# One-hot and gate rows of the expert layers in float16 pairs, built on VectorE alone

## The chip, the cores and the metric

The kernel runs on one NeuronCore of a Trainium2 chip. The metric is device time in microseconds, the median of the runs. TensorE (PE in the profile) multiplies matrices into PSUM; VectorE (DVE), ScalarE (ACT) and GpSimd (POOL) work on SBUF tiles of 128 partitions, the first two on PSUM too; SyncE (SP) issues the loads of the weights. Each engine takes its instructions in one fixed order and waits at semaphores for the others.

## The reference, cut to what matters

The program is a stack of a dozen phases over 256 tokens of width 1024: feed-forward layers, four kinds of attention and state-space mixers, and, twice, a layer of 16384 experts. The change lies in the two expert layers alone:

```python
def peer_ffn(x, norm_g, q_w, sub_keys, u, v):
    ...
    h = rmsnorm(x, norm_g).reshape(T, D)
    q = (h @ q_w).reshape(T, PEER_HEADS, 2, PEER_HALF)
    s = jnp.einsum('thcd,ckd->thck', q, sub_keys).astype(jnp.float32)
    s1, i1 = lax.top_k(s[:, :, 0], PEER_TOPK)
    s2, i2 = lax.top_k(s[:, :, 1], PEER_TOPK)
    cand_s = (s1[..., :, None] + s2[..., None, :]).reshape(T, PEER_HEADS, PEER_TOPK * PEER_TOPK)
    cand_i = (i1[..., :, None] * N_KEYS + i2[..., None, :]).reshape(T, PEER_HEADS, PEER_TOPK * PEER_TOPK)
    best_s, best_pos = lax.top_k(cand_s, PEER_TOPK)
    idx = jnp.take_along_axis(cand_i, best_pos, axis=-1)
    gate = jax.nn.softmax(best_s, axis=-1).astype(x.dtype)
    ...
        a = jnp.einsum('nd,nhkd->nhk', hb, u[ib])
        w = gb * jax.nn.gelu(a, approximate=False)
        return jnp.einsum('nhk,nhkd->nd', w, v[ib])
```

For each token, 8 heads choose 16 experts each out of 128 x 128, and the gated gelu of the token's product with row `u` of an expert weighs row `v` of it.

## The kernel before

The weights stream in once, in units of 128 x 1024 float32. SP loads a unit into a buffer `raw`; ACT rounds it to float32r (`whi`, L189) and DVE takes the remainder (`wlo`, L190), so that three matmuls give a product of nearly float32 precision. `Stream.conv` does both, and a unit's field `eng` can put the remainder on another engine: in each expert layer `peer_units` sets it to GpSimd for 24 units (`us[LO0:LO1:LOS]`, every second one of units 24 to 71).

The experts are not gathered. The layer computes gelu(h . u) for all 16384 experts, multiplies by a dense gate (zero for an expert that was not chosen), and multiplies by all of v. `W[i1, i2, token]`, with i1 on the partitions, holds the gated values; it lies in three tiles, `Wa` (i2 0 to 63), `Wc` (64 to 79) and `Wb` (80 to 127), with the 256 tokens innermost. What happens in a layer, in the order of the code:

- 16 units of the query weights are multiplied (`chunk_t`), and x scaled by the norm's factor is transposed for the expert products (`scaled`, the tile `hn`).
- `u_pair(i)` takes two units, 24 matmuls of 256 columns for each (L1672 to L1674), then a gelu on ACT. 58 such pairs run with background work beside them, four more after it, ahead of and among the products with v. If some tokens' gates are there already, the gelu goes to a tile `ga` and `flush` (L1661) multiplies it into `W`; for the other tokens it is written to `W`.
- Beside these products runs the generator `search()`, the background work. `half_scores` finds the 16 best keys per half and head (MAX8, FIND_INDEX8 and MATCH_REPLACE8 on DVE); `choose` forms the candidates, finds the 16 best and softmaxes them, and turns the chosen i1, i2 and the gates so that (head, rank) lies on the partitions and tokens along the free axis (`key2`, `gate2`); `gates` builds the dense gates. For a pair of tokens it compares a row 0 to 127 with both keys (`eq`, L1588: 512 float16 values in a partition: key half, token, place) and multiplies the one-hot row of i1 by both parts of the gate (`A`, split into a float16 and the remainder). Of the four pairs in eight tokens, `HOT = "gaga"` gives the first and third product `A` to GpSimd (one instruction, L1600), the second and fourth to ACT (four instructions, L1597). Two matmuls a token, `A` times the one-hot row of i2 (L1607), give the token's 128 x 128 gates in PSUM. For eight tokens at a time `meet` multiplies those into the gelu values that are in `W` (DVE, L1575), or writes them where no gelu is yet (ACT, L1578).

What stands around what is set by credits. Each unit of `u_pair` calls `tick(UTICK)`, which runs the generator until its yielded weights have used up the credit. DVE keeps the order of the code up to the end of `choose` (a region of manual schedule); after that, and on the other engines throughout, a scheduler places instructions by its own estimates within the limits of the data and of buffers (four `eq`, four `A`, four `raw`). After the 58 pairs `drain_bg` runs what is left of the generator.

Of the kernel before, what the change touches and what calls it, by code (L numbers as in the profile page):

```python
# [33 lines left out]
# columns of the per-partition parameter tile  # L34
# [11 lines left out]
# rows of the parameters that are spread over the partitions  # L46
# [29 lines left out]
HOT = "gaga"  # L76
# the gates are split into float16 parts at this scale
# [33 lines left out]
class Stream:  # L111
    """the weights in the order of their use: loaded ahead, then split into float32r parts ahead.
    A phase that has room lends a pool for more parts; its last units always lie there, so that the
    first ones of the next phase can be split before the last ones of this are used up"""
# [38 lines left out]
    def place(self, u):  # L153
        """the pool for the parts of u, or None when there is no room yet"""
# [42 lines left out]
    def take(self, n=1, conv=True):  # L197
        """the next n units, held until the next call"""
# [15 lines left out]
class HTs:  # L214
    """blocks of eight in several tiles"""
# [8 lines left out]
class Next:  # L224
    """the transposed normed x for a phase, in hi and lo parts, without the tokens' factors r"""
# [15 lines left out]
    def trans(self, t):  # L241
        """pairs of blocks alternate between two banks, which the splits take in turns"""
# [27 lines left out]
class Kern:  # L270
# [34 lines left out]
    def tri(self, pool, name, dtype, n, keep, other, base, step, mult):  # L305
        """value keep where mult*partition + step*free + base >= 0, else other"""
# [25 lines left out]
    def split(self, src, shape, tag, pool, bufs=1):  # L332
        """hi and lo parts of src, each exact in float32r"""
# [16 lines left out]
    def rstd(self, out, ss, n, eps, mul=1.0, ms=None):  # L350
        """mul * (ss / n + eps) ** -0.5; ms is for what is raised to the power"""
# [16 lines left out]
    def begin(self, pool):  # L368
        """the transposed normed x of this phase; its first token tile is prepared by now"""
# [47 lines left out]
    def second(self, nx, pool):  # L417
        """the second token tile of the norm"""
# [29 lines left out]
    def chunk_n(self, acc, ht, units, kb0, nk, t, cols):  # L448
        """natural orientation: acc[:, t, :cols] gets h[t] @ W"""
# [10 lines left out]
    def nat(self, acc, ht, cols, head=None, mid=None, tick=0):  # L460
        """natural orientation, a chunk of four units with two k-blocks each"""
# [17 lines left out]
    def wide(self, accs, ht, nk, head=None, mid=None, tail=None):  # L479
        """accs[t][:, half, :] gets h[t] @ W for the 1024 columns of W; units hold one k-block"""  # L480
# [32 lines left out]
    def chunk_t(self, acc, ht, nk, kb0, units):  # L513
        """transposed orientation: acc[:, b // 2, (b % 2) * 256 :] = (h @ W_b)^T for four blocks b"""
# [15 lines left out]
    def log_exp_table(self):  # L530
        """the table with both functions, loaded once the last activation noted is issued"""
# [6 lines left out]
    def traced(self):  # L538
        """the instruction traced last"""
# [1446 lines left out]
```

## Time and profile before

| | |
|---|---|
| time, median of 3 runs (lowest, highest) | 3185.92 us (3181.03, 3186.96) |
| span of the profiled execution | 3172.1 us |
| busy: PE, DVE, ACT, POOL | 3031.7, 2231.7, 1724.8, 541.6 us |
| first expert layer: first key search to its last gate | 1270 to 1735 us of the span |
| second expert layer, the same | 2285 to 2746 us |

The profile's span is from the first to the last instruction on the core; the device time has some 14 us more around it. Busy times are unions of records on an engine; a share near 100% in a stretch says that the engine has no gap there. All times in the traces are from the span's start.

### The profile page before, as it was taken

The numbers are of one execution on the slowest core, as the hardware profiler recorded it, in microseconds if no ns is written. First come the engines' busy times: TensorE is split into PE (matmuls) and PEld (weight loads), VectorE is DVE, ScalarE is ACT, GpSimd is POOL, SyncE is SP. The second block draws the span as 40 slices with busy tenths as digits, with TensorE's granted clock in tenths as the row PEclk, the third lists the DMA queues.
The fourth block names the chain that finished last, engine by engine and source line by source line (L and its number), as shares of the span: only waits on it lengthen the run. The fifth ranks groups of instructions, "written<-read, shape, count | busy, mean of one in ns | idle before, by whom it ended". The sixth has DMA issues, their size and how long they took to land. (4 is left out here: it accounts for less than half of the span.)

```text
span 3172.1 us, 48810 instructions
## 1 busy us (share of the span) xinstructions
PE 3031.7 (96%) x18398; PEld 2625.6 (83%) x18398; DVE 2231.7 (70%) x3555; ACT 1724.8 (54%) x2976; POOL 541.6 (17%) x391
## 2 busy tenths in 40 slices
PE   8999999999999999988988999998998898999998
PEld 7888888887888988988988888886898888888886
DVE  5555655547655776999998555567699999855555
ACT  5446545437545656445766444456544676544444
POOL 0000000002000012133665000001123466400000
PEclk9999999999999999999999999999999999999999
DMA  7653555653554544544444666664354444566664
GB/s 228 184 185 110 179 185 186 186 168 107 180 184 140 176 123 133 162 145 149 139 132 134 187 187 187 188 182 150 109 160 146 148 135 133 154 188 189 186 186 149
DMA packets 142221, 513.66 MB, mean 162 GB/s; under 512 B 16672, under 2 KB 17312, under 8 KB 141984
## 3 DMA queue, kind: packets, MB, share of 16 engines
q1 hardware_dynamic: 138816, 504.16, 52.1%
q10 hardware_dynamic: 3168, 6.37, 0.6%
q8 instruction: 144, 2.36, 0.3%
q14 instruction: 93, 0.76, 0.1%
HBM read 509.42 MB, written 1.05 MB: 161 GB/s over the span
## 5 line engine op out<-in xcount | busy, mean ns | idle before, releaser
L190 DVE TENSOR_TENSOR wlo<-raw,whi 128x1024 fp32r<-128x1024 f32 x912 | 1164.8, 1281 | 547.5 <-ACT whi L189 546.1
L189 ACT CAST whi<-raw 128x1024 fp32r<-128x1024 f32 x962 | 1001.9, 1046 | 697.6 <-PE tr L1673 199.7
L1674 PE MATMUL tr<-hs,wlo 128*128 128x256 f32 x1984 | 566.6, 286 | 39.4 <-DVE wlo L190 39.4
L1672 PE MATMUL tr<-hs,whi 128*128 128x256 f32 x1984 | 574.8, 290 | 5.8 <-DVE gate L1554 4.5
L1673 PE MATMUL tr<-hs,whi 128*128 128x256 f32 x1984 | 563.1, 284 | 0.0
L1674 PEld LDWEIGHTS tr<-hs,wlo 128*128 128x128 f32 x1984 | 377.4, 190 | 44.8 <-DVE wlo L190 44.8
L328 PE MATMUL acc<-whi,wh 128*128 128x512 f32 x1024 | 406.0, 396 | 0.0
L330 PE MATMUL acc<-whi,wl 128*128 128x512 f32 x1024 | 405.9, 396 | 0.0
L329 PE MATMUL acc<-wlo,wh 128*128 128x512 f32 x1024 | 405.9, 396 | 0.0
L1672 PEld LDWEIGHTS tr<-hs,whi 128*128 128x128 f32 x1984 | 379.2, 191 | 7.0 <-issue 3.7
L1673 PEld LDWEIGHTS tr<-hs,whi 128*128 128x128 f32 x1984 | 379.3, 191 | 0.1
L328 PE MATMUL acc<-whi,ht 128*128 128x512 f32 (+2 forms) x832 | 330.1, 397 | 3.8 <-ACT ht L258 3.8
L329 PE MATMUL acc<-wlo,ht 128*128 128x512 f32 (+2 forms) x832 | 326.6, 393 | 1.2 <-DVE wlo L190 1.1
L330 PE MATMUL acc<-whi,ht 128*128 128x512 f32 (+2 forms) x832 | 325.8, 392 | 0.0
L1600 POOL TENSOR_TENSOR A<-eq,gate 128x512 f16<-128x512 f16 x128 | 239.8, 1883 | 206.8 <-DVE eq L1588 197.4
L330 PEld LDWEIGHTS acc<-whi,wl 128*128 128x128 f32 x1024 | 192.9, 188 | 47.0
L329 PEld LDWEIGHTS acc<-wlo,wh 128*128 128x128 f32 x1024 | 192.9, 188 | 46.9
L328 PEld LDWEIGHTS acc<-whi,wh 128*128 128x128 f32 x1024 | 192.9, 188 | 46.8
L1588 DVE TENSOR_TENSOR eq<-iof,key 128x512 f16<-128x512 f16 x256 | 204.3, 833 | 20.2 <-PE acc L1607 19.1
L328 PEld LDWEIGHTS acc<-whi,ht 128*128 128x128 f32 x832 | 157.1, 189 | 37.8 <-ACT ht L258 4.6
L1597 ACT ACTIVATE A<-eq,gate 128x128 f16<-128x128 f16 x512 | 163.1, 393 | 46.4 <-DVE eq L1588 46.2
L329 PEld LDWEIGHTS acc<-wlo,ht 128*128 128x128 f32 x832 | 157.1, 189 | 35.9 <-DVE wlo L190 3.2
(430 smaller groups left out, 4955.2 us busy)
## 6 DMA issues: line engine op xcount, KB each, us to landing
raw<-in_peer_u_dram SPq DMA_DIRECT2D x256, 512.0 KB, 3.6
raw<-in_peer_v_dram SPq DMA_DIRECT2D x256, 512.0 KB, 3.6
raw<-in_ffn_in_dram SPq DMA_DIRECT2D x176, 512.0 KB, 3.6
raw<-in_ffn_out_dram SPq DMA_DIRECT2D x88, 512.0 KB, 3.5
raw<-in_ssm_zx_dram SPq DMA_DIRECT2D x48, 512.0 KB, 3.6
raw<-in_peer_q_dram SPq DMA_DIRECT2D x32, 512.0 KB, 3.7
raw<-in_sb_qk_dram SPq DMA_DIRECT2D x16, 512.0 KB, 4.5
raw<-in_ssm_out_dram SPq DMA_DIRECT2D x16, 512.0 KB, 3.6
```

The lines of the kernel that those rows point to most:

```text
L189: nc.scalar.copy(hi[:, : u.n], raw[:, : u.n])
L190: (u.eng or nc.vector).tensor_tensor(lo[:, : u.n], raw[:, : u.n], hi[:, : u.n].bitcast(F32), ALU.subtract)
L328: mm(out, lh, rh, start=start, stop=False, skip_group_check=True)
L329: mm(out, lh, rl, start=False, stop=False, skip_group_check=True)
L330: mm(out, ll, rh, start=False, stop=stop, skip_group_check=True)
L1588: v.tensor_tensor(eq, iof.unsqueeze(1).unsqueeze(1).broadcast_to([P, 2, 2, P]), key2[:, :, n : n + 2].unsqueeze(3).broadcast_to([P, 2, 2, P]),
L1597: nc.scalar.activation(A[:, i, k, :], eq[:, 0, i, :], AF.Copy, scale=gate2[:, k, n + i : n + i + 1])
L1600: (nc.gpsimd if way == "g" else v).tensor_tensor(A, eq[:, 0].unsqueeze(2).broadcast_to([P, 2, 2, P]), gate2[:, :, n : n + 2].rearrange("p ...
L1672: mm(out, u.hi[:, k, :], hs.hi[:, k, :], start=k + b == 0, stop=False, **kw)
L1673: mm(out, u.hi[:, k, :], hs.lo[:, k, :], start=False, stop=False, **kw)
L1674: mm(out, u.lo[:, k, :], hs.hi[:, k, :], start=False, stop=k == KD - 1, **kw)
```

## The change

`key2` and `gate2` become one float16 tile `kg` of four rows (both keys, both parts of the gate). The one-hot tiles get the two tokens of a pair innermost: `[2, 128 places, 2 tokens]`, so the keys and gates are read as runs of two neighbouring float16 values, no longer as one value repeated along the row. All `A` products are on DVE, and so are the remainders of the 24 units, the multiplication in `flush`, and `hn`. The matmuls read `A` and `eq` with a step of two values. `meet` runs with the tokens innermost: `W` is touched in runs of eight float32 values, and PSUM is read with a step of 128 values. The weights that pace the generator are new: `UTICK` 1.3 to 2.0, and other yields throughout.

```diff
-UTICK = 1.3
-MEET = lambda nc: nc.gpsimd
-GW = 2.6
-CW = 1.0
-HOT = "gaga"
+UTICK = 2.0
+GW = 3.9
...
-        for u in us[LO0:LO1:LOS]:
-            u.eng = self.nc.gpsimd
...
-            key2 = p.tile([P, 2, S], F16, name="key2")
-            gate2 = p.tile([P, 2, S], F32, name="gate2")
+            kg = p.tile([P, 4, S], F16, name="kg")
...
-                            yield 0.9
+                            yield 1.65
...
-                            yield CW * 0.9
+                            yield 1.4
...
-                            yield CW * 0.9
+                            yield 2.0
...
-                            yield CW * 0.9
+                            yield 1.0
...
-                    v.tensor_copy(key2[:, :, ts], tr[:, 0:256].rearrange("p (a b) -> p a b", a=2))
-                    gh = tk.tile([P, P], F16, tag="gh", bufs=1, name="gh")
-                    v.tensor_scalar(gh, tr[:, 256:384], GSCALE, None, ALU.mult)
-                    v.tensor_copy(gate2[:, 0, ts], gh)
-                    v.scalar_tensor_tensor(gate2[:, 1, ts], tr[:, 256:384], GSCALE, gh,
+                    v.tensor_copy(kg[:, 0:2, ts], tr[:, 0:256].rearrange("p (a b) -> p a b", a=2))
+                    v.tensor_scalar(kg[:, 2, ts], tr[:, 256:384], GSCALE, None, ALU.mult)
+                    v.scalar_tensor_tensor(kg[:, 3, ts], tr[:, 256:384], GSCALE, kg[:, 2, ts],
...
-                iof = hot.tile([P, P], F16, name="iof")
+                iof = hot.tile([P, P, 2], F16, name="iof")
...
-                    gv = gp.rearrange("p h (n i) -> p (h n) i", i=P)
+                    gv = gp.rearrange("p h (n i) -> p i (h n)", i=P)
...
-                            w = W(b0, m)[:, :, ns].rearrange("p i n -> p n i")
-                            v.scalar_tensor_tensor(w, gv[:, :, b0:m], 1 / GSCALE, w, ALU.mult,
+                            w = W(b0, m)[:, :, ns]
+                            v.scalar_tensor_tensor(w, gv[:, b0:m, :], 1 / GSCALE, w, ALU.mult,
                                                    ALU.mult)
...
-                        eq = hot.tile([P, 2, 2, P], F16, tag="eq", bufs=NB, name="eq")
+                        eq = hot.tile([P, 2, P, 2], F16, tag="eq", bufs=NB, name="eq")
                         v.tensor_tensor(
-                            eq, iof.unsqueeze(1).unsqueeze(1).broadcast_to([P, 2, 2, P]),
-                            key2[:, :, n : n + 2].unsqueeze(3).broadcast_to([P, 2, 2, P]),
+                            eq, iof.unsqueeze(1).broadcast_to([P, 2, P, 2]),
+                            kg[:, 0:2, n : n + 2].unsqueeze(2).broadcast_to([P, 2, P, 2]),
                             ALU.is_equal)
-                        A = hot.tile([P, 2, 2, P], F16, tag="A", bufs=NA, name="A")
...
-                                    nc.scalar.activation(A[:, i, k, :], eq[:, 0, i, :], AF.Copy,
-                                                         scale=gate2[:, k, n + i : n + i + 1])
...
-                            (nc.gpsimd if way == "g" else v).tensor_tensor(
-                                A, eq[:, 0].unsqueeze(2).broadcast_to([P, 2, 2, P]),
...
+                        A = hot.tile([P, 2, P, 2], F16, tag="A", bufs=NA, name="A")
+                        v.tensor_tensor(
+                            A, eq[:, 0].unsqueeze(1).broadcast_to([P, 2, P, 2]),
+                            kg[:, 2:4, n : n + 2].unsqueeze(2).broadcast_to([P, 2, P, 2]),
+                            ALU.mult)
...
-                                mm(o, A[:, i, k, :], eq[:, 1, i, :], start=k == 0, stop=k == 1,
+                                mm(o, A[:, k, :, i], eq[:, 1, :, i], start=k == 0, stop=k == 1,
...
-                nc.gpsimd.tensor_scalar(hs.src[t], self.x[:, t, :], ht.r[:, t : t + 1], None,
+                v.tensor_scalar(hs.src[t], self.x[:, t, :], ht.r[:, t : t + 1], None,
...
-                    MEET(nc).tensor_tensor(w, ga, w, ALU.mult)
+                    v.tensor_tensor(w, ga, w, ALU.mult)
```

The order that the built programs have shows the move at three places. On DVE, in `choose`, for one head of the second token tile before (wlo is a unit's remainder, eq<-pf,io the comparison that looks up the chosen ranks; `eq<-iof` further down is the one-hot row):

```order
L190 TENSOR_TENSOR wlo<-raw,whi 128x1024
L1509 MAX best<-cs 128x8
L1510 MAX_INDEX pu<-best,cs 128x8
L1511 MATCH_REPLACE c_13279<-best,cs 128x50
L1512 MAX best<-c_13279 128x8
L1513 MAX_INDEX pu<-best,c_13279 128x8
L1514 CAST pf<-pu 128x16
L1517 TENSOR_TENSOR eq<-pf,io 128x800
L1520 TENSOR_TENSOR eq<-eq,ci 128x800
L1525 TENSOR_REDUCE idx<-eq 128x16
L190 TENSOR_TENSOR wlo<-raw,whi 128x1024
```

and after:

```order
L182 TENSOR_TENSOR wlo<-raw,whi 128x1024
L1515 TENSOR_REDUCE idx<-eq 128x16
L182 TENSOR_TENSOR wlo<-raw,whi 128x1024
L1499 MAX best<-cs 128x8
L1577 TENSOR_TENSOR eq<-iof,kg 128x512
L1500 MAX_INDEX pu<-best,cs 128x8
L1501 MATCH_REPLACE c_13811<-best,cs 128x50
L1582 TENSOR_TENSOR A<-eq,kg 128x512
L1502 MAX best<-c_13811 128x8
L1503 MAX_INDEX pu<-best,c_13811 128x8
L1504 CAST pf<-pu 128x16
L182 TENSOR_TENSOR wlo<-raw,whi 128x1024
```

Every second remainder of these units was on POOL; now all are on DVE, two or three a head, and the first pairs of tokens (those of the first token tile) are built between them. From the first key search to the last key row, DVE before has 37 remainders and POOL 24; after, DVE has 71. From there to the last `meet` it is 63 before and 55 after.

On DVE in `gates`, one group of eight tokens before:

```order
L1588 TENSOR_TENSOR eq<-iof,key_10964 128x512 x2
L190 TENSOR_TENSOR wlo<-raw,whi 128x1024
L1588 TENSOR_TENSOR eq<-iof,key_10964 128x512 x2
L1575 SCALAR_TENSOR_TENSOR Wa<-acc,Wa 128x8x64
L190 TENSOR_TENSOR wlo<-raw,whi 128x1024
L1575 SCALAR_TENSOR_TENSOR Wc<-acc,Wc 128x8x16
L1575 SCALAR_TENSOR_TENSOR Wb<-acc,Wb 128x8x32
```

and after:

```order
L1577 TENSOR_TENSOR eq<-iof,kg 128x512
L1564 SCALAR_TENSOR_TENSOR Wa<-acc,Wa 128x64x8
L1582 TENSOR_TENSOR A<-eq,kg 128x512
L182 TENSOR_TENSOR wlo<-raw,whi 128x1024
L1564 SCALAR_TENSOR_TENSOR Wc<-acc,Wc 128x16x8
L1577 TENSOR_TENSOR eq<-iof,kg 128x512 x2
L1582 TENSOR_TENSOR A<-eq,kg 128x512 x2
L1577 TENSOR_TENSOR eq<-iof,kg 128x512 x2
L182 TENSOR_TENSOR wlo<-raw,whi 128x1024
L1643 TENSOR_TENSOR Wb<-ga,Wb 128x2x176
L1564 SCALAR_TENSOR_TENSOR Wb<-acc,Wb 128x30x8
```

A group still has two units' remainders; four `A` products and one multiplication of `flush` (every other unit) came in.

On PE, at the last one-hot matmuls of the first layer before (acc<-eq,A is the one-hot product, tr<-hs the expert products):

```order
L1607 LDWEIGHTS A
L1607 MATMUL acc<-eq,A 128x128
L1607 LDWEIGHTS A
L1607 MATMUL acc<-eq,A 128x128
L1672 MATMUL tr<-hs,whi 128x256
L1673 MATMUL tr<-hs,whi 128x256
L1674 MATMUL tr<-hs,wlo 128x256
```

and after, in the same layer (acc<-whi,wh is the product with v):

```order
L1589 LDWEIGHTS A
L1589 MATMUL acc<-eq,A 128x128
L1589 LDWEIGHTS A
L1589 MATMUL acc<-eq,A 128x128
L320 MATMUL acc<-whi,wh 128x512 x2
L1656 MATMUL tr<-hs,wlo 128x256
L1654 MATMUL tr<-hs,whi 128x256
```

Before, 144 matmuls of expert products (six units) follow the last one-hot product ahead of the first product with v; after, two matmuls with v follow at once and then 46 of expert products (two units). The last 56 one-hot matmuls have only 50 expert products between them, where the stretch before that has 24 for each eight.

More of the change, by code (lines that the diff above doesn't have):

```diff
@@ L1526, in choose @@
                                             ALU.add)
-                            yield CW * 0.9
+                            yield 1.0
                     dif = tk.tile([P, 8, 16], F32, tag="dif", bufs=1, name="dif")
@@ L1535, in choose @@
                     v.tensor_tensor(dif, dif, zz.unsqueeze(2).broadcast_to([P, 8, 16]), ALU.mult)
-                    yield CW * 0.6
+                    yield 0.9
                     ix = tk.tile([P, 3, P], I32, tag="ix", bufs=1, name="ix")
@@ L1542, in choose @@
                     v.tensor_copy(fx, ix[:, 0:2, :])
-                    yield CW * 0.6
+                    yield 0.9
                     tr = self.tr()
@@ L1549, in choose @@
                     ts = slice(t * P, (t + 1) * P)
-                    v.tensor_copy(key2[:, :, ts], tr[:, 0:256].rearrange("p (a b) -> p a b", a=2))
-                    gh = tk.tile([P, P], F16, tag="gh", bufs=1, name="gh")
-                    v.tensor_scalar(gh, tr[:, 256:384], GSCALE, None, ALU.mult)
-                    v.tensor_copy(gate2[:, 0, ts], gh)
-                    v.scalar_tensor_tensor(gate2[:, 1, ts], tr[:, 256:384], GSCALE, gh,
+                    v.tensor_copy(kg[:, 0:2, ts], tr[:, 0:256].rearrange("p (a b) -> p a b", a=2))
+                    v.tensor_scalar(kg[:, 2, ts], tr[:, 256:384], GSCALE, None, ALU.mult)
+                    v.scalar_tensor_tensor(kg[:, 3, ts], tr[:, 256:384], GSCALE, kg[:, 2, ts],
                                            ALU.mult, ALU.subtract)
-                    yield CW * 0.4
+                    yield 0.9
             def gates():
                 nonlocal built
-                iof = hot.tile([P, P], F16, name="iof")
-                nc.gpsimd.iota(iof, pattern=[[1, P]], base=0, channel_multiplier=0,
+                iof = hot.tile([P, P, 2], F16, name="iof")
+                nc.gpsimd.iota(iof, pattern=[[1, P], [0, 2]], base=0, channel_multiplier=0,
                                allow_small_or_imprecise_dtypes=True)
@@ L1573, in meet @@
                         if b0 < m:
[L1574 to L1575 removed]
+                            w = W(b0, m)[:, :, ns]
+                            v.scalar_tensor_tensor(w, gv[:, b0:m, :], 1 / GSCALE, w, ALU.mult,
                                                    ALU.mult)
                         if m < b1:
[L1578 to L1579 removed]
+                            nc.scalar.activation(W(m, b1)[:, :, ns], gv[:, m:b1, :], AF.Copy,
+                                                 scale=1 / GSCALE)
                     built = n0 + 8
@@ L1586, in gates @@
                         n = n0 + j
-                        eq = hot.tile([P, 2, 2, P], F16, tag="eq", bufs=NB, name="eq")
+                        eq = hot.tile([P, 2, P, 2], F16, tag="eq", bufs=NB, name="eq")
                         v.tensor_tensor(
-                            eq, iof.unsqueeze(1).unsqueeze(1).broadcast_to([P, 2, 2, P]),
-                            key2[:, :, n : n + 2].unsqueeze(3).broadcast_to([P, 2, 2, P]),
+                            eq, iof.unsqueeze(1).broadcast_to([P, 2, P, 2]),
+                            kg[:, 0:2, n : n + 2].unsqueeze(2).broadcast_to([P, 2, P, 2]),
                             ALU.is_equal)
-                        A = hot.tile([P, 2, 2, P], F16, tag="A", bufs=NA, name="A")
-                        way = HOT[j // 2]
-                        if way == "a":
-                            for i in range(2):
-                                for k in range(2):
-                                    nc.scalar.activation(A[:, i, k, :], eq[:, 0, i, :], AF.Copy,
-                                                         scale=gate2[:, k, n + i : n + i + 1])
-                        else:
-                            (nc.gpsimd if way == "g" else v).tensor_tensor(
-                                A, eq[:, 0].unsqueeze(2).broadcast_to([P, 2, 2, P]),
-                                gate2[:, :, n : n + 2].rearrange("p k n -> p n k").unsqueeze(3)
-                                .broadcast_to([P, 2, 2, P]), ALU.mult)
+                        A = hot.tile([P, 2, P, 2], F16, tag="A", bufs=NA, name="A")
+                        v.tensor_tensor(
+                            A, eq[:, 0].unsqueeze(1).broadcast_to([P, 2, P, 2]),
+                            kg[:, 2:4, n : n + 2].unsqueeze(2).broadcast_to([P, 2, P, 2]),
+                            ALU.mult)
                         for i in range(2):
@@ L1743, in peer @@
                         tail = self.add_x(
-                            accs, gate2.rearrange("p a b -> p (a b)").bitcast(BF16))
+                            accs, kg.rearrange("p a b -> p (a b)").bitcast(BF16))
                         self.open_region()
```

11 lines of the change are left out of this document (1 added, 10 removed).

## The prediction, as it was put on record

> **What bounds the kernel now.** I read the page first, then the stretches of the first expert layer, then who waits for whom in it, then DVE's groups in two of its stretches.
>
> ```profile
> span 3172.1 us, 48810 instructions
> PE 3031.7 (96%) x18398; PEld 2625.6 (83%) x18398; DVE 2231.7 (70%) x3555; ACT 1724.8 (54%) x2976; POOL 541.6 (17%) x391
> ```
>
> PE is idle for 140 us in all. The windows say where; columns are the stretch, its length, and busy time with counts on PE, PEld, DVE, ACT, POOL.
>
> ```profile
> 1235.00:1270.20 35.20, 35.20 (x242) 32.40 (x241) 21.39 (x43) 25.19 (x52) 9.70 (x8) 1.00 0.38 115
> 1270.20:1304.80 34.60, 34.60 (x294) 34.60 (x293) 34.36 (x168) 15.62 (x17) 0.00 (x0) 1.00 0.54 162
> 1304.80:1406.10 101.30, 90.12 (x738) 88.48 (x737) 94.51 (x241) 43.29 (x51) 35.05 (x14) 1.00 0.50 157
> 1406.10:1480.70 74.60, 63.14 (x505) 61.22 (x503) 72.47 (x142) 31.59 (x42) 27.55 (x12) 0.98 0.44 141
> 1480.70:1735.10 254.40, 225.88 (x2055) 219.72 (x2054) 237.67 (x270) 178.85 (x425) 153.31 (x92) 0.98 0.46 135
> 1735.10:1752.70 17.60, 17.60 (x138) 17.06 (x137) 10.52 (x11) 8.31 (x12) 6.61 (x4) 1.00 0.62 178
> 1760.00:1940.00 180.00, 180.00 (x812) 146.71 (x811) 104.41 (x126) 86.52 (x126) 1.84 (x1) 1.00 0.63 187
> ```
>
> From 1270 to 1735 PE stands 51 us while DVE is 93 to 99% busy: DVE is the bound there. The second layer's stretches read alike (three of its four rows):
>
> ```profile
> 2319.40:2420.70 101.30, 90.10 (x737) 88.46 (x737) 94.51 (x241) 43.24 (x51) 35.09 (x14) 1.00 0.51 156
> 2420.70:2495.20 74.50, 63.06 (x505) 61.20 (x503) 72.38 (x142) 31.52 (x42) 27.55 (x12) 0.98 0.43 142
> 2495.20:2745.80 250.60, 225.00 (x2060) 218.93 (x2058) 237.77 (x271) 179.48 (x425) 148.07 (x92) 0.99 0.46 136
> ```
>
> PE stands 48 us there, so some 99 of the 140 us lie where the change is. Outside (first and last rows) PE has no gap. Call 1270 to 1480.7 the search (210.5 us) and 1480.7 to 1735.1 the gates (254.4 us). PE's waits from 1270 to 1755:
>
> ```profile
> PE acc L1607 <- POOL A L1600: 26.8, 18, 3.7
> PE tr L1674 <- DVE wlo L190: 19.7, 13, 1.8
> ```
>
> The first is POOL's latency on top of a full DVE, the second DVE itself. DVE's groups in the search (line, tiles, shape, count | busy us, mean ns):
>
> ```profile
> L190 DVE TENSOR_TENSOR wlo<-raw,whi 128x1024 fp32r<-128x1024 f32 x38 | 58.1, 1530 | 1.0 <-ACT whi L189 1.0
> L1514 DVE CAST pf<-pu 128x16 f32<-128x16 uint32 x16 | 19.0, 1190 | 0.6
> L1517 DVE TENSOR_TENSOR eq<-pf,io 128x800 f32<-128x800 f32 x16 | 18.0, 1125 | 0.3
> L1493 DVE TENSOR_TENSOR cs<-tv 128x16 f32<-128x16 f32 (+5 forms) x16 | 5.1, 388 | 0.0
> ```
>
> and in the gates:
>
> ```profile
> L1588 DVE TENSOR_TENSOR eq<-iof,key 128x512 f16<-128x512 f16 x124 | 100.0, 842 | 9.9 <-PE acc L1607 9.3
> L190 DVE TENSOR_TENSOR wlo<-raw,whi 128x1024 fp32r<-128x1024 f32 x64 | 91.8, 1434 | 5.4 <-ACT whi L189 4.9
> L1575 DVE SCALAR_TENSOR_TENSOR Wa<-acc,Wa 128x512 f32<-128x512 f32 (+4 forms) x32 | 41.5, 1298 | 1.4 <-PE acc L1607 1.4
> L1575 DVE SCALAR_TENSOR_TENSOR Wc<-acc,Wc 128x128 f32<-128x128 f32 (+7 forms) x27 | 9.8, 363 | 0.0
> L1575 DVE SCALAR_TENSOR_TENSOR Wb<-acc,Wb 128x288 f32<-128x288 f32 (+17 forms) x19 | 9.2, 482 | 0.0
> ```
>
> These sum to 252 us in 254. Eight tokens cost DVE 4 x 0.842 + 2 x 1.434 + 1.9 of meets = 8.1 us, and 31 groups of that fill the stretch.
>
> **What POOL costs DVE.** The same instructions where POOL is idle (1760 to 1940), two lines' min/median/max, one shape of the small additions alone, and two more DVE rows for prices:
>
> ```profile
> L190 DVE TENSOR_TENSOR wlo<-raw,whi 128x1024 fp32r<-128x1024 f32 x65 | 79.6, 1225 | 37.4 <-ACT whi L189 37.4
> L343 DVE TENSOR_TENSOR wl<-Wa,wh 128x256 fp32r<-128x256 f32 x58 | 24.7, 425 | 36.8 <-ACT wh L342 36.8
> ...
> L1514 DVE CAST pf<-pu x32: 174/1182/2395, 1342.9 to 2484.3; 128x16 f32<-128x16 uint32 x32
> L1588 DVE TENSOR_TENSOR eq<-iof,key x256: 671/687/1572, 1406.2 to 2737.6; 128x512 f16<-128x512 f16 x128
> ...
> L1493 DVE TENSOR_TENSOR cs<-tv 128x16 f32<-128x16 f32 x6 | 0.7, 167 | 0.0
> ...
> L343 DVE TENSOR_TENSOR hidl<-tr,hidh 128x512 fp32r<-128x512 f32 x44 | 30.0, 683 | 0.0
> L1071 DVE TENSOR_SCALAR hn<-x,r 128x1024 f32<-128x1024 f32 x2 | 1.5, 758 | 0.0
> ```
>
> A remainder falls from 1.43-1.53 to 1.225 us, a cast from 1.19 to 0.174. POOL's and ACT's work that moves or goes (1240 to 1755, then 1270 to 1755):
>
> ```profile
> L1600 POOL TENSOR_TENSOR A<-eq,gate 128x512 f16<-128x512 f16 x64 | 121.5, 1908 | 101.9 <-DVE eq L1588 97.2 <-DVE gate L1554 4.7
> L190 POOL TENSOR_TENSOR wlo<-raw,whi 128x1024 fp32r<-128x1024 f32 x24 | 59.6, 2485 | 151.8 <-ACT whi L189 151.8
> L1661 POOL TENSOR_TENSOR Wb<-ga,Wb 128x512 f32<-128x512 f32 (+18 forms) x22 | 33.8, 1538 | 21.1 <-ACT ga L1682 13.0 <-ACT Wb L1578 8.1
> L1653 POOL TENSOR_SCALAR hn<-x,r 128x1024 f32<-128x1024 f32 x2 | 7.8, 3920 | 0.2
> ...
> L1597 ACT ACTIVATE A<-eq,gate 128x128 f16<-128x128 f16 x256 | 81.6, 393 | 23.3 <-DVE eq L1588 23.2
> ```
>
> **The search, per layer.** DVE loses the delays: 38 x 0.305 = 11.6 us on remainders, 16 x 1.016 = 16.3 on casts, 16 x 0.134 = 2.1 on the comparison and as much on the product behind it, some 7 on 32 small additions (up to 0.22 each): 39 us. Four old pairs go (3.4). It gains 71 - 38 = 33 remainders x 1.225 = 40.4 us, of which 24 come from POOL and the rest because more units stand in this stretch now, and 17 `eq` and `A` plus one meet, 7.9 at the prices below. Net +6 us on 210.5, with DVE at 201 busy now. PE gets ten units more there: 71 x 24 matmuls at 0.12 us (next rows) is 204, with transposes and key products some 212. Both engines are about full; I take 218 us.
>
> ```profile
> 1562.58 0.28 PE L1673 MATMUL tr<-hs,whi 128*128 128x256 f32 x1
> 1562.70 0.28 PE L1674 MATMUL tr<-hs,wlo 128*128 128x256 f32 x1
> 1562.83 0.62 PE L1607 MATMUL acc<-eq,A 128*128 128x128 f16 x8
> 1563.26 0.36 PE L1672 MATMUL tr<-hs,whi 128*128 128x256 f32 x1
> ```
>
> **The gates, per layer.** No row of before shows DVE on pairs. Price of an `eq` or `A` in the new form: at best two values a cycle, which makes it as long as the 256-element row, 0.425 us; at worst as long as now without POOL, 0.687. The old `eq` repeats one key along the row, and at 0.687 it takes one element at a time like the float32 row of 512 (0.683); the new one reads neighbours everywhere, so I take 0.425. The Trainium skill, "VectorE: DVE Perf Modes", section "What auto-detection actually checks", says the same: two elements a cycle for a two-source operation if every tensor is 16-bit with step 1; no run here shows it yet, and by the other price the sum would turn to a loss (first rival).
>
> Price of a 512-element meet: at best the 0.683 of the 512-element row that reads PSUM, at worst the 1.298 it has now. At present PSUM is read in order and `W` with a step of 1 KB, and it costs twice an ordinary row; after, `W` is in order by eight and PSUM has the step. I take 0.69, as the only slow thing seen is the step in SBUF. The smaller meets shrink alike, to about 0.28 (`Wc`) and, for three groups in four, 0.36 (`Wb`).
>
> `flush`, by the built order 26 in this stretch, of 216 elements on average: 0.38 each, a little under the 256-element row (bounds: that row, and a third of it). So a group of eight tokens: 8 x 0.425 + 2 x 1.225 + 0.69 + 0.28 + 0.27 + 0.31 = 7.4 us of DVE, where it was 8.1. PE needs 2 x 24 x 0.12 + 16 x 0.054 (eight one-hot matmuls in 0.43 us above) = 6.6. DVE stays the bound by 0.8. Thirty groups are left; 26.5 run with two units each, 196 us, and the last 3.5, which have two units between them all, take 3.5 x 4.9 + 2.4 = 19.5. Then PE's order has a product with v directly behind the last one-hot product, so it waits for the last meet, a round on ACT and back, 2 us, and has 46 expert products left, 5.5. Sum 223 us, against 254.4 and the 14.8 that six units take up to the first v product, 1735.1 to 1749.9:
>
> ```profile
> 1749.88 0.39 PE L328 MATMUL acc<-whi,wh 128*128 128x512 f32 x1
> ```
>
> **What costs nothing.** The ten late `flush` (0.683) fall where DVE is 104 of 180 us busy. `hn` at 0.758 for 3.92 us lies under a PE that is full (1235 to 1270). ACT loses 82 us, but is 179 of 254 busy and decides nothing. A cast of the gate row goes, twice a layer. No transfer moves: SP's 512 KB units need no more than the 187 GB/s of 1760 to 1940. Strided reads by PE: at best free, at worst the 0.12 us pace of a float32 matmul in place of 0.054, which makes a group 7.7 on PE, 0.3 over DVE, 8 us a layer; a step of 4 bytes is a float32 row's own, so I take nothing.
>
> **The sum.** A layer falls from 210.5 + 254.4 + 14.8 = 479.7 to 218 + 223 = 441, 39 us; two layers 78. That stands against the profiled execution's 3172.1 of span and 14 around it, which is the median of 3185.9. Forecast: 3108 us. Its own range is 3070 to 3140: from 58 a layer, all of PE's gaps and some more cadence, to 23 where small losses at buffers eat half.
>
> **Rivals.** *Slower: pairs run one value a cycle.* `eq` and `A` at 0.687 make a group 9.5 us and the tail longer (3.5 x 7 + 2.4): 4 more in the search, 60 more in the gates, 505 a layer, 25 over before: 3237 us. It decides from about 0.58 us an instruction on (39 us over 256 is 0.15). For it: 512 float16 take as long as 512 float32 in every row so far. Against: the repeated key is reason enough for that. *Less gained: the step moves from `W` to PSUM and the meets stay at 1.3.* Some 0.85 a group and in the tail, 25 to 27 us a layer, and 12 to 14 are left of the gain: 3159 us. For it: something in a stepped read halves the rate now, and nothing excludes PSUM. By the skill's "Advanced Engine Details and Errata", section "Memory Cachelines", two consecutive float32 in PSUM should be contiguous for best throughput; it says that of matmuls, and by that rule the time would be these 3159; no run here has a stepped PSUM read by DVE. *No change: PE's order.* PE's and DVE's rows are set ahead by a scheduler; if its estimates of `eq` and `A` are off, PE waits at the one-hot products for DVE as it did for POOL (26.8 us a layer), and with the four buffers DVE runs only eight tokens ahead; with 12 more lost in the search the 39 are gone: 3186, give or take 6.
>
> **Chances.** Forecast 0.55 (faster), meets as slow as now 0.25 (faster), no change 0.06, pairs at full length 0.14 (slower). Leaving out the last two, 0.2, the range is 3070 to 3168. Within 0.2%, about 6 us, counts as no change (the three runs lie 6 us apart). Faster 0.81, same 0.05, slower 0.14.
>
> **What the next profile would show.** Right: `eq<-iof` and `A` near 0.42 us, 128 each a layer; meets of 512 near 0.69; `pf` near 0.17 and remainders at 1.22 throughout; no PE wait for POOL; gates about 215 us from the last key row to the last meet with DVE still over 90% busy; search a few us longer. Wrong: `eq` near 0.69, or meets at 1.3, or PE idle before L1589 for more than 20 us a layer.

## The result, and the profile after

The changed kernel takes 3096.94 us, median of 4 runs (3084.48 to 3097.53), where the kernel before takes 3183.86 (3181.03 to 3186.96) on the same chip: a ratio of 0.9726, 95% interval 0.9709 to 0.9744, 87 us less. The forecast was 3108 us, 78 less. The profiled execution took 3097.53 us with a span of 3095.8. From the page:

```profile
span 3095.8 us, 48085 instructions
PE 3037.2 (98%) x18398; PEld 2629.8 (85%) x18398; DVE 2137.7 (69%) x3941; ACT 1557.9 (50%) x2440; POOL 78.8 (3%) x139
```

Next the stretches after, columns as in the prediction (then granted clock, DMA share, GB/s): first key search to last key row (the search), from there to the last meet (the gates), 60 us of that by themselves, and the products with v; below them the same cuts of before.

```profile
1269.40:1493.10 223.70, 217.59 (x1799) 214.95 (x1798) 205.63 (x599) 102.25 (x117) 0.00 (x0) 0.99 0.56 168
1493.10:1693.30 200.20, 198.04 (x1866) 194.57 (x1866) 186.16 (x408) 88.02 (x153) 0.00 (x0) 1.00 0.50 150
1560.00:1620.00 60.00, 60.00 (x570) 59.12 (x570) 57.21 (x126) 26.37 (x43) 0.00 (x0) 1.00 0.51 152
1693.20:2072.50 379.30, 378.41 (x1677) 307.61 (x1678) 222.94 (x271) 180.49 (x265) 1.51 (x1) 1.00 0.63 187
```

```profile
1270.20:1482.30 212.10, 187.93 (x1532) 184.30 (x1530) 202.93 (x553) 91.69 (x110) 62.60 (x26) 0.99 0.48 152
1482.30:1735.10 252.80, 225.81 (x2053) 219.72 (x2054) 236.07 (x267) 177.65 (x423) 153.31 (x92) 0.98 0.46 135
1749.90:2120.90 371.00, 371.00 (x1633) 300.56 (x1632) 214.72 (x258) 178.22 (x260) 5.78 (x4) 1.00 0.64 187
```

The second and third figure of a row tell the story: PE stood 24.2 + 27.0 us in search and gates before and stands 6.1 + 2.2 after. From the first key search to the last product with v the first layer fell from 850.6 to 803.1 us, the second from 846.4 to 804.8: 89.1 together. The two spans differ by only 76.3, because 13.6 us were lost between the layers, at a place that the change doesn't touch (see the clock, below). Within the layers the clock did not make the gain: TensorE's clock is at half there for 23.9 us before and 20.5 us after.

DVE's groups after, in the gates, then two in the search, and the cast by itself (min/median/max):

```profile
L182 DVE TENSOR_TENSOR wlo<-raw,whi 128x1024 fp32r<-128x1024 f32 x55 | 67.0, 1219 | 3.8 <-ACT whi L181 3.7
L1582 DVE TENSOR_TENSOR A<-eq,kg 128x512 f16<-128x512 f16 x120 | 48.2, 417 | 0.3
L1577 DVE TENSOR_TENSOR eq<-iof,kg 128x512 f16<-128x512 f16 x119 | 46.0, 420 | 9.9 <-PE acc L1589 9.1
L1564 DVE SCALAR_TENSOR_TENSOR Wa<-acc,Wa 128x512 f32<-128x512 f32 x31 | 21.1, 682 | 0.0
...
L182 DVE TENSOR_TENSOR wlo<-raw,whi 128x1024 fp32r<-128x1024 f32 x72 | 87.5, 1216 | 8.0 <-ACT whi L181 7.9
L1507 DVE TENSOR_TENSOR eq<-pf,io 128x800 f32<-128x800 f32 x16 | 15.8, 985 | 0.1
...
L1504 DVE CAST pf<-pu x32: 164/174/176, 1366.9 to 2458.8; 128x16 f32<-128x16 uint32 x32
```

Every price moved where the prediction put it: the pairs at 0.42 us, the 512-element meet at 0.68, the remainder at 1.22, the cast at 0.174. PE's waits have shrunk. Its largest ones from 1269 to 1711, and the one wait of DVE for PE, follow:

```profile
PE tr L1654 <- ACT Wa L1667: 2.0, 3, 0.7
PE tr L1656 <- DVE wlo L182: 1.8, 4, 0.9
PE acc L320 <- ACT wh L334: 1.8, 1, 1.8
PE acc L1589 <- DVE A L1582: 1.4, 3, 0.6
...
DVE eq L1577 <- PE acc L1589: 9.1, 23, 0.8
```

No wait for POOL is left (26.8 us before), and none sums to more than 2 us. DVE's wait for PE to give `eq` buffers back is as long as before (9.3 us), in 23 pieces and not 10; what has gone is PE's own waiting. In the gates TensorE is the bound: the 60 us above hold no gap of PE. DVE's timeline shows by how much; one group of eight tokens, `Wa` meet to `Wa` meet (start, us, operation):

```profile
1564.32 0.68 DVE L1564 SCALAR_TENSOR_TENSOR Wa<-acc,Wa 128x512 f32<-128x512 f32 x1
1564.92 0.28 DVE L1564 SCALAR_TENSOR_TENSOR Wc<-acc,Wc 128x128 f32<-128x128 f32 x1
1565.23 0.76 DVE L1577 TENSOR_TENSOR eq<-iof,kg 128x512 f16<-128x512 f16 x2
1565.91 0.42 DVE L1582 TENSOR_TENSOR A<-eq,kg 128x512 f16<-128x512 f16 x1
1566.25 1.22 DVE L182 TENSOR_TENSOR wlo<-raw,whi 128x1024 fp32r<-128x1024 f32 x1
1567.38 0.32 DVE L1643 TENSOR_TENSOR Wb<-ga,Wb 128x160 f32<-128x160 f32 x1
1567.62 0.20 DVE L1564 SCALAR_TENSOR_TENSOR Wb<-acc,Wb 128x48 f32<-128x48 f32 x1
1567.74 0.42 DVE L1582 TENSOR_TENSOR A<-eq,kg 128x512 f16<-128x512 f16 x1
1568.63 0.76 DVE L1577 TENSOR_TENSOR eq<-iof,kg 128x512 f16<-128x512 f16 x2 [0.48 <-PE acc L1589]
1569.31 0.42 DVE L1582 TENSOR_TENSOR A<-eq,kg 128x512 f16<-128x512 f16 x1
1569.65 1.22 DVE L182 TENSOR_TENSOR wlo<-raw,whi 128x1024 fp32r<-128x1024 f32 x1
1570.78 0.42 DVE L1582 TENSOR_TENSOR A<-eq,kg 128x512 f16<-128x512 f16 x1
1571.12 0.68 DVE L1564 SCALAR_TENSOR_TENSOR Wa<-acc,Wa 128x512 f32<-128x512 f32 x1
```

A group takes 6.80 us, 0.48 of them a wait for PE. Read start to start, not by durations: an `A` of 0.42 us is followed after 0.34, a remainder of 1.22 after 1.13. Most records overlap the next by some 0.08 us, so the 14 instructions cost 6.3 us and not the 7.4 of the prediction. The rows of before had it already: five groups of DVE in the gates sum to 252 us, where the window's busy time is 237.67.

### The profile page after: what moved, and what is told of

Same layout as the page of the kernel before. It is cut to its first block, busy times and chain, and to the rows that moved or that the text cites. A ratio compares the mean times of both kernels' runs of the same rounds, so it can differ in the third digit from the quotient of the medians.

```text
span 3095.8 us, 48085 instructions
## 1 busy us (share of the span) xinstructions
PE 3037.2 (98%) x18398; PEld 2629.8 (85%) x18398; DVE 2137.7 (69%) x3941; ACT 1557.9 (50%) x2440; POOL 78.8 (3%) x139
## 4 chain that ended last, share of the span: by engine, by line
PE 52%; DVE 5%; ACT 2%; issue 1%; POOL 0%; DMA 0%; DVEq 0%; POOLq 0%; ACTq 0%
PE acc L321 9%; PE acc L322 9%; PE acc L320 9%; PE tr L1654 7%; PE tr L1656 7%; PE tr L1655 6%; DVE wlo L182 2%; PE acc L1589 2%; PE acc L520 1%; PE acc L519 1%; PE acc L518 1%; ACT whi L181 1%; DVE idx L1515 0%; DVE eq L1507 0%; PE acc L1376 0%
## 5 line engine op out<-in xcount | busy, mean ns | idle before, releaser
L1655 PEld LDWEIGHTS tr<-hs,whi 128*128 128x128 f32 x1984 | 379.3, 191 | 0.1
L320 PEld LDWEIGHTS acc<-whi,ht 128*128 128x128 f32 x832 | 156.9, 189 | 37.8 <-ACT ht L250 4.6
L322 PEld LDWEIGHTS acc<-whi,ht 128*128 128x128 f32 x832 | 156.6, 188 | 35.4 <-DVE ht L253 1.1
L334 ACT CAST wh<-Wa 128x256 fp32r<-128x256 f32 x128 | 51.7, 407 | 176.4 <-PE acc L321 175.6
L320 PE MATMUL acc<-whi,hidh 128*128 128x512 f32 x352 | 138.9, 395 | 0.0
```

The costliest lines, as they stand in the source:

```text
L320: mm(out, lh, rh, start=start, stop=False, skip_group_check=True)
L322: mm(out, ll, rh, start=False, stop=stop, skip_group_check=True)
L334: nc.scalar.copy(hi, src)
L1655: mm(out, u.hi[:, k, :], hs.lo[:, k, :], start=False, stop=False, **kw)
```

## The experiments

The theory: the gain has three parts, (1) the meets in order, (2) the remainders and casts that no longer run beside POOL, (3) the pairs, without which the products that come to DVE would eat the gain. The rivals: the pairs bring nothing and POOL's absence is the whole, or POOL should have kept part of the work. The table gives every run. Each ratio is to the kernel before as it ran beside that one, where its median was 3178 to 3185 us. "Layers" is the time from the first key search to the last product with v in the profiled execution, first layer, second layer. It is the steadier measure, since it leaves the stretch between the layers out.

| kernel | median us (lowest, highest) | ratio to before, 95% interval | layers, us |
|---|---|---|---|
| before (in the prediction) | 3185.92 (3181.03, 3186.96) | 1 | 850.6, 846.4 |
| after (above) | 3096.94 (3084.48, 3097.53) | 0.9726 [0.9709, 0.9744] | 803.1, 804.8 |
| before, remainders on DVE | 3160.91 (3153.42, 3169.76) | 0.9936 [0.9916, 0.9957] | 837.3, 838.1 |
| before, new meet | 3138.98 (3126.24, 3139.32) | 0.9858 [0.9835, 0.9881] | 826.5, 825.0 |
| before, both | 3109.97 (3103.59, 3116.63) | 0.9779 [0.9750, 0.9807] | 815.8, 814.9 |
| after, one token at a time | 3201.22 (3198.29, 3210.85) | 1.0061 [1.0037, 1.0086] | 861.5, 860.6 |
| after, old meet | 3135.03 (3129.26, 3142.10) | 0.9853 [0.9822, 0.9884] | 823.8, 822.5 |
| after, half of `A` on POOL | 3117.50 (3115.45, 3129.86) | 0.9821 [0.9793, 0.9850] | 820.1, 819.3 |
| after, 24 remainders on POOL | 3084.03 (3081.73, 3086.20) | 0.9694 [0.9670, 0.9717] | 804.7, 803.2 |
| the same again | 3085.76 (3083.90, 3097.14) | 0.9720 [0.9699, 0.9741] | 803.2, 804.7 |
| after, again | 3084.84 (3081.15, 3086.29) | 0.9698 [0.9684, 0.9712] | 805.0, 802.9 |
| after, a third time | 3090.70 (3083.86, 3097.69) | 0.9719 [0.9692, 0.9745] | 803.0, 804.8 |
| after, old spreading | 3082.54 (3076.10, 3089.61) | 0.9688 [0.9664, 0.9711] | 798.9, 798.9 |
| the same again | 3088.10 (3073.86, 3090.59) | 0.9708 [0.9682, 0.9733] | 798.9, 798.9 |

**Are the pairs what pays?** The changed kernel with one token's row after another, so that a key stands repeated along the row as before; all else as after.

```diff
-eq = hot.tile([P, 2, P, 2], F16, ...)
+eq = hot.tile([P, 2, 2, P], F16, ...)
...
-    kg[:, 0:2, n : n + 2].unsqueeze(2).broadcast_to([P, 2, P, 2])
+    kg[:, 0:2, n : n + 2].unsqueeze(3).broadcast_to([P, 2, 2, P])
...
-mm(o, A[:, k, :, i], eq[:, 1, :, i], ...)
+mm(o, A[:, i, k, :], eq[:, 1, i, :], ...)
```

> The changed kernel with eq and A again as rows of one token, each key and gate repeated along 128 places (all still on VectorE, matmuls read in order). Theory (pairs halve the instruction, and VectorE becomes the bound without that): eq and A near 0.687 us instead of 0.42, 69 us more of VectorE a layer, of which some 14 find slack; 45 to 60 us a layer slower than the changed kernel, 3190 to 3215 us, slower than before. Rival (the layout hardly matters, freeing GpSimd made the gain): 3097 to 3115 us.

It is slower than the kernel before, as expected. Its gates, and DVE's two groups there:

```profile
1505.70:1751.10 245.40, 213.17 (x1848) 196.85 (x1846) 236.90 (x395) 89.41 (x153) 0.00 (x0) 0.97 0.42 122
...
L1582 DVE TENSOR_TENSOR A<-eq,kg 128x512 f16<-128x512 f16 x112 | 73.2, 683 | 0.0
L1577 DVE TENSOR_TENSOR eq<-iof,kg 128x512 f16<-128x512 f16 x112 | 72.9, 683 | 0.7 <-PE acc L1589 0.7
```

0.683 against 0.418 us, which are the lengths of the 512-element and the 256-element row of before (0.683 and 0.425). DVE is the bound again, PE idle for 32 us. To put all `A` on DVE is a loss without the pairs; the layout takes 56 to 58 us off a layer. By estimate at most 8 of these come by way of the clock: it is at half for 54.6 us in the two layers here and for 20.5 in the changed kernel.

**The meets.** The changed kernel with the old access of `meet`, and the old kernel with the new one alone (the lines of `meet` for ACT, not shown, change alike):

```diff
-gv = gp.rearrange("p h (n i) -> p i (h n)", i=P)
+gv = gp.rearrange("p h (n i) -> p (h n) i", i=P)
...
-w = W(b0, m)[:, :, ns]
-v.scalar_tensor_tensor(w, gv[:, b0:m, :], 1 / GSCALE, w, ...)
+w = W(b0, m)[:, :, ns].rearrange("p i n -> p n i")
+v.scalar_tensor_tensor(w, gv[:, :, b0:m], 1 / GSCALE, w, ...)
```

> The changed kernel with meet again reading PSUM in order and touching W with a step of 1 KB. Theory (the step in W doubles a meet, and VectorE has only some 14 us of slack a layer in the gates): 512-element meets near 1.3 us, 27 us more of VectorE a layer, 12 to 20 us a layer slower, 3120 to 3137 us. Rival (TensorE is the bound now and hides it): 3097 us, give or take 5.

> The kernel before with only meet changed (tokens innermost). Theory (VectorE's work bounds the gates): a 512-element meet near 0.69 us, 25 us less of VectorE a layer, 10 to 25 us a layer faster, 3135 to 3165 us. Rival (TensorE's waits for the A products of GpSimd are a bound of their own): less than 5 us a layer, 3175 to 3185 us.

In time both lie in the ranges expected. By layers the first costs 20.7 and 17.7 us where 12 to 20 were forecast; the first of these layers is at half clock for 17.1 us, the changed kernel's for 6.8. The 512-element meet with the old access in the new kernel, its gates, and the meet and `eq` in the old kernel with the new access:

```profile
1494.00:1714.40 220.40, 204.53 (x1866) 197.69 (x1866) 210.90 (x409) 91.43 (x154) 0.00 (x0) 0.98 0.46 136
...
L1564 DVE SCALAR_TENSOR_TENSOR Wa<-acc,Wa 128x512 f32<-128x512 f32 x31 | 41.3, 1332 | 0.0
```

```profile
L1588 DVE TENSOR_TENSOR eq<-iof,key 128x512 f16<-128x512 f16 x124 | 109.5, 922 | 8.2 <-PE acc L1607 8.2
...
L1575 DVE SCALAR_TENSOR_TENSOR Wa<-acc,Wa 128x512 f32<-128x512 f32 (+4 forms) x32 | 21.6, 674 | 0.6 <-PE acc L1607 0.6
...
PE acc L1607 <- POOL A L1600: 6.6, 19, 0.6
```

1.332 against 0.682 and 1.298 against 0.674: it is the step of 1 KB in `W` that costs, and PSUM read with a step of 512 bytes costs nothing (the row of before that reads 512 values of PSUM in order takes 0.683). In the new kernel DVE is 24.7 us busier in the gates and these are 20.2 us longer: of the 14 us that DVE had been idle there, only 4.5 took up the work. On the old kernel it is worth 24 and 21 us a layer, more than the 32 x 0.62 = 20 of the large meets, as the smaller meets shrink too. The wait for POOL's `A` falls from 26.8 us to 6.6, though POOL makes the same products at 1.67 us each (1.92 before): most of that wait probably hung on how late DVE came with the `eq` that POOL needs (18 waits shorter by 0.25 us would be 4.5 of the 20 us), where the prediction had booked it as POOL's latency on top of a full DVE.

**The remainders.** The old kernel with no remainder on POOL; the same with the new meet:

```diff
-LO1 = 72
+LO1 = 24
```

> The kernel before, only with the 24 remainders of GpSimd a layer on VectorE. Theory (a GpSimd remainder delays VectorE by about what it takes off it: 39 us of delays against 29 us of work a layer): 0 to 10 us a layer faster, 3164 to 3186 us. Rival (the work moved to GpSimd was saved in full): 25 to 29 us a layer slower, 3234 to 3242 us.

> The kernel before with both single parts: meet with the tokens innermost, and the 24 remainders a layer on VectorE; A stays with GpSimd and ACT, eq as it was. Theory (both parts shorten one engine, VectorE, that stays the bound; 24 and 41 us alone): they add up, 60 to 70 us faster, 3112 to 3122 us. Rival (without one of them TensorE's waits for A on GpSimd take over): under 50 us, above 3132 us.

The first gave 24 us where at most 20 were expected, the second 68. The search of the first, and the cast there:

```profile
1268.00:1470.10 202.10, 190.69 (x1548) 187.23 (x1547) 193.76 (x581) 93.90 (x118) 7.28 (x5) 0.97 0.52 160
...
L1514 DVE CAST pf<-pu 128x16 f32<-128x16 uint32 x16 | 3.3, 208 | 0.6
```

With 24 remainders more in hand DVE is 9 us less busy in the search (193.8 against 202.9): 24 x 1.22 = 29 came, some 38 of delays went (39 in the prediction). The cast fell from 1190 to 208 ns with nothing else changed, so the delay came from POOL's remainders beside it. By layers the parts add up: 21.6 (remainders) and 45.5 (meets) make 67.1, both together gave 66.3 of the change's 89.1. The clock has a share in these differences: it is at half in the two layers for 23.9 us before, and for 37.5, 3.4 and 17.1 us with remainders, meets and both. With half of that taken out, an estimate, the parts are 28 and 35 and both together 63, so they still add up. The other 23 are what the pairs bring after the products that came to DVE are paid, less some 10 that the new spreading costs (below). `flush` and `hn`, which moved too, were not tried by themselves.

**Should POOL keep something?** The changed kernel with the 24 remainders on POOL as before; with the first and third `A` of a group on POOL, in the new layout.

```diff
+        for u in us[24:72:2]:
+            u.eng = self.nc.gpsimd
```

```diff
-v.tensor_tensor(A, ...)
+(v if j // 2 % 2 else nc.gpsimd).tensor_tensor(A, ...)
```

> The changed kernel, only with the same 24 remainders a layer back on GpSimd. Theory (as for the kernel before: delays of 39 us on VectorE for 29 us taken off it): 0 to 12 us a layer slower, 3097 to 3121 us, with casts near 1.2 us again. Rival (GpSimd relieves a VectorE that is still close to the bound in the search): 3 to 6 us a layer faster, 3085 to 3091 us.

> The changed kernel with two of each four A products on GpSimd, in the pair layout. Theory (GpSimd's latency and its delays on VectorE come back, while VectorE's relief of 27 us a layer is worth nothing beside a full TensorE): TensorE waits for A again, 5 to 20 us a layer slower than the changed kernel's 3085 at full clock, 3095 to 3125 us. Rival (float16 pairs on GpSimd cost nobody anything): 3080 to 3090 us.

The remainders on POOL gave 3084 us, which looked like a gain of 13 where a loss was expected. Its layers (804.7, 803.2) were those of the changed kernel (803.1, 804.8), so the 13 us lay elsewhere. Both ran again:

> The changed kernel once more. Its profile had one stretch of 27 us at half the TensorE clock, 77 us after the last product with v of the first expert layer, and three of four runs took 3097 us, the fourth, with a higher mean clock, 3084. Theory (the stretch comes and goes from run to run, whatever the kernel): both times again, 3084 and 3097 us, give or take 4. Rival (it belongs to this kernel): all near 3097.

> The changed kernel with 24 remainders a layer on GpSimd, once more, beside the changed kernel. Its search and gates took as long as the changed kernel's, and all its runs lacked the stretch at half clock. Theory (chance of the runs): now some runs have the stretch, and runs of equal clock are equal to the changed kernel's within 3 us. Rival (GpSimd's share of the work keeps the clock up or saves time): all runs near 3084, 12 us under the changed kernel's median.

The changed kernel alone then took 3084.84, all five runs within 3081 to 3086, and the other spread from 3083.90 to 3097.14: both times come with either kernel, and there is no difference. DVE still pays for POOL here, a cast 685 ns (less than the 1.2 us expected) and the comparison behind it 1257 in place of 985 (the search, then two groups in it):

```profile
1271.30:1495.80 224.50, 215.63 (x1794) 213.70 (x1793) 194.82 (x567) 102.22 (x117) 61.08 (x24) 1.00 0.56 167
...
L1509 DVE TENSOR_TENSOR eq<-pf,io 128x800 f32<-128x800 f32 x16 | 20.1, 1257 | 0.2
...
L1506 DVE CAST pf<-pu 128x16 f32<-128x16 uint32 x16 | 11.0, 685 | 0.5
```

but it has 24 remainders less to do and is 194.8 us busy in the search, 10.8 less than in the changed kernel. The search is no shorter for it, 224.5 us against 223.7. With `A` on POOL it is a plain loss, 14 to 17 us a layer, within the 5 to 20 expected. PE's wait and two of DVE's groups in the gates:

```profile
PE acc L1589 <- POOL A L1582: 11.3, 13, 1.8
...
L182 DVE TENSOR_TENSOR wlo<-raw,whi 128x1024 fp32r<-128x1024 f32 x55 | 88.1, 1601 | 9.6 <-ACT whi L181 9.6
L1577 DVE TENSOR_TENSOR eq<-iof,kg 128x512 f16<-128x512 f16 x120 | 62.7, 558 | 2.1 <-PE acc L1589 1.5
```

POOL takes 60 products of 0.42 us off DVE, and the remainder rises by 0.38 us and `eq` by 0.14: 55 x 0.38 + 120 x 0.14 = 38 us for the 25 that are saved.

**The spreading.** The changed kernel with the old weights of the generator:

```diff
-UTICK = 2.0
-GW = 3.9
+UTICK = 1.3
+GW = 2.6
...
-                            yield 1.65
+                            yield 0.9
```

(and eight more yields back to their old values).

> The changed kernel with the weights of the kernel before (UTICK 1.3, GW 2.6 and the old yields). Ten units fewer stand beside the search, six follow the gates. Theory (TensorE is the bound now, and only a search as dense as before makes it wait): some 16 us a layer of TensorE gaps in the search in place of 6, none more in the gates; 4 to 10 us a layer slower, 3105 to 3117 us against 3097 of like clock. Rival (pacing is worth nothing): within 4 us of the changed kernel.

> The changed kernel with the spreading of the units and the group's width in cost as they were before the change, a second time and beside the changed kernel on one chip. Theory: the earlier spreading puts more expert matmuls into the search and the gates, where TensorE then hardly pauses, so the short stretches at half clock go and the first v product waits for nothing: first key search to last v 799 us in either layer against 803 to 805, in all about 3076 us without the long half-clock stretch between the layers, 3089 with it, some 8 us (0.25%) under the changed kernel in the same condition. Rival: the difference was one of the runs; both kernels then stand within 3 us, and the two layers take 803 us or more here too.

> The changed kernel itself, on the same chip as the version with the earlier spreading. Both theories: 3084 us without the long half-clock stretch between the layers, 3097 with it, first key search to last v 803 to 805 us in each layer. By the theory it is the slower of the two by about 8 us in the same condition, by the rival it is equal within 3 us.

My first expectation fell: 4 to 10 us a layer slower was forecast, and the layers are 4 to 6 us faster, 798.9 in each of the four that were profiled. The second run of it, and the changed kernel beside it on the same chip (the gates, then the whole of the first layer):

```profile
1467.70:1682.00 214.30, 214.30 (x2006) 211.32 (x2005) 196.20 (x411) 96.65 (x174) 0.00 (x0) 1.00 0.53 159
...
1270.10:2069.00 798.90, 791.27 (x5338) 714.50 (x5338) 613.72 (x1270) 371.73 (x546) 1.51 (x1) 1.00 0.57 173
```

```profile
1269.90:2072.90 803.00, 793.79 (x5338) 717.19 (x5338) 614.73 (x1275) 370.62 (x534) 1.51 (x1) 1.00 0.57 172
```

The old weights put more expert products into the gates (2006 matmuls against 1866), where PE now has no gap at all, and fewer into the search, where DVE is the busier. The same 5338 matmuls take 2.5 us less busy time, as no stretch at half clock lies in them, and 1.6 us of gaps go. The medians of the two, 3088 and 3091, overlap in their runs, since each kernel's runs lie in two clusters. The mean granted clock of a run tells them apart: 3073.9 to 3076.2 us at 0.998 and 3087.3 to 3090.6 at 0.992 or 0.993 with the old spreading, 3081.2 to 3086.3 at 0.994 to 0.996 and 3096.7 to 3097.7 at 0.989 to 0.991 with the new, of which one run, 3090.70 at 0.993, lies between. By like clusters the old spreading is some 8 us faster, of all the versions here the fastest.

## Why the prediction was right, and where not

- **Pairs at 0.425 us: right** (0.418). By the Trainium skill, "VectorE: DVE Perf Modes", section "What auto-detection actually checks", two-byte operands with step 1 go at two elements a cycle; the trace agrees, and the repeated key in the one-token layout took 0.683.
- **Meets at 0.69: right** (0.682). The rival held the step in PSUM to be as bad as that in SBUF. The Trainium skill's "Advanced Engine Details and Errata", section "Memory Cachelines", has a penalty for SBUF when each access hits another 16-byte line, and with that 1.298 against 0.682 agrees; what it says of PSUM and matmuls does not carry over to DVE's reads here.
- **POOL's cost on DVE: right.** Remainder 1.22 throughout, cast 0.174. Strided reads by PE: the one-hot matmul kept its pace (its records are 218 ns at the median, 219 before), nothing lost.
- **Search, 218 us: too short by 5.7.** Of this 1.6 is the cut: the last key row of before ends at 1482.3, and the prediction cut at 1480.7. DVE was put at 207 us of work (201 and 6 more) and PE at 212; they have 205.6 and 217.6. So PE's term was too small, and the stretch is 6 us longer than its busier engine, as forecast.
- **Gates: the bound was named wrong.** "DVE stays the bound by 0.8" rested on durations added up, 7.4 us a group. The records overlap by some 0.08 us an instruction; DVE needs 6.3 and PE sets the pace: 64 matmuls of 570 in 60 us are 6.74, where the prediction had 6.6. So 26.5 groups take 179 us, not 196. What is left of the 200.2 us for the tail and the wait, 21.5, is what was forecast for them (19.5 + 2), and the gates with that wait take 200.2 us, not 217.5. DVE is 93% busy there, as it was before; the prediction took "over 90%" for the sign of a bound, and it is none, with PE at 99%.
- **46 products left over:** 8.3 us (379.3 - 371.0) against 5.5; a stretch of 3.4 us at half clock (1.7) and a gap of PE (0.9) lie there too.
- **A layer: 441 forecast, 432 measured** (223.7 + 200.2 + 8.3), the second 434: 89 us in two layers and not 78.
- **The base was 12 us too high.** The prediction, like the text ahead of it, set the profile's 3172.1 of span and "14 around it" against the median. The runs since show 1.7 us around a span (3097.53 against 3095.8). The profile of before was of an execution without the long stretch at half clock between the layers (3170 to 3173 us in five other runs with its mean clock of 0.994); the runs near the median have a mean clock of 0.988 to 0.991, as the runs after with that stretch have, and the profile after shows it; no profile of the kernel before has caught it. Both errors made the forecast too high: against the runs without the stretch (3174 - 89 = 3085) by 23 us, 12 from the base and 11 from the gain. Against the medians, which by their clock have the stretch on both sides, only the gain's error is left: 3108 for 3097. That the median of four runs fell there was luck: later medians of the same kernel were 3084.84 and 3090.70.

That the gain rests on PE's gaps, and that DVE was the bound before, is shown by the experiments: in the old kernel each part that took time off DVE took it off the layers, and giving DVE 0.265 us more on each of 512 products (136 us) in the new one lost 114. Once PE is the bound it holds no longer: 24 remainders taken off DVE again made it 10.8 us less busy in the search and changed nothing in the time.

## What to carry to other kernels

Put the loop's short dimension innermost when a value must be repeated along a row: a run of two neighbouring float16 values was enough to bring VectorE's 512 values from 0.68 to 0.42 us. Between the two, a step cost less on the PSUM side than in SBUF (0.68 against 1.3 us for a meet). Before GpSimd is given a share of VectorE's work, price what its instruction does to VectorE's own beside it; a small cast took up to 2.4 us beside a remainder of 2.5 there. To find which engine is the bound, read the records start to start and not by their durations. When an engine gets faster, set the interleaving by the next engine's gaps, here TensorE's, and measure it: here the old weights were the better ones.

## What the runs showed of the hardware that I had not expected

TensorE's granted clock falls to half for stretches of 3.4 us or multiples of it, shortly after a gap in its work. The changed kernel: the gap ahead of the first product with v, the stretch 3.7 us later, and the long one between the layers.

```profile
1691.30:1693.10 1.80, 0.04 (x1) 0.00 (x0) 1.80 (x6) 0.61 (x3) 0.00 (x0) 1.00 0.00 0
1695.00:1698.40 3.40, 3.40 (x17) 3.40 (x17) 3.40 (x6) 0.60 (x1) 0.00 (x0) 0.50 0.64 176
...
2149.00:2176.30 27.30, 27.02 (x74) 14.06 (x75) 13.19 (x41) 11.38 (x44) 0.00 (x0) 0.50 0.25 78
```

The same piece of the program in the changed kernel's second profile, whose execution took 3085.51 us, and then the 3.4 us ahead of it in the first profile and in the second:

```profile
2150.60:2177.90 27.30, 26.90 (x137) 16.45 (x137) 19.02 (x70) 18.61 (x71) 0.00 (x0) 1.00 0.25 78
```

```profile
2145.60:2149.00 3.40, 1.98 (x14) 1.60 (x14) 3.40 (x15) 3.40 (x6) 0.00 (x0) 1.00 0.44 165
```

```profile
2146.20:2149.60 3.40, 2.22 (x17) 1.74 (x16) 3.02 (x13) 3.02 (x4) 0.00 (x0) 1.00 0.72 234
```

74 matmuls against 137 in as many microseconds: half a stretch of 27.3 us is the 13.6 us between the layers, and the distance between the two clusters of runs. It stands there after gaps of 3.74 and 1.18 us, in some runs of the kernel and not in others. The clock records of the traces tell more. In each of the 14 profiles all starts lie on one grid of 3.413 us, and a stretch fills whole windows of that grid. What counts most is how long PE stands within one window. Between 20 and 3055 us of the spans, all 68 windows at full clock in which PE stood for more than 2 us had half clock in the next one, and none of the 12072 with less than 1.3 us had; from 1.3 to 2 us it was 28 of 128 (the six gaps of 1.53 us in the search of before had none). So the same gaps bring a stretch or not by where they fall on the grid, which differs from run to run. Between the layers, the window ahead of the long stretch holds 1.3 to 1.7 us of idle PE in the eight profiles that have that stretch; in the six that lack it, that window holds 1.2. What decides in the range from 1.3 to 2 us, and why the long stretch lasts 27 us or more while PE is busy, stays open. The Trainium skill, "TensorE: Matmul & The Clock Gate", section "Part 1: The HAM clock gate (the "warmup" mystery)", tells of a free-running window of 3413 ns and half rate after an idle window. The length and the grid agree with every stretch here, but here a window idle for little more than half of it was enough.

The short stretches are the likely cause of most of what the old spreading gains: the changed kernel has 20.5 us of them in the two layers, the other none, and PE is busy for 2.5 and 4.8 us less there with the same matmuls, of 10 us gained. No run took a gap away by itself, so this is argued from the traces.
